# The second norm in six steps per quarter, and DVE alone draining the banks between the halves, in a two-layer flow-matching step

## The chip, the cores and the metric

The kernel runs on one core of a Trainium2 chip. The metric is the time of one execution in microseconds (us) on the device; the median of several executions counts. The engines have short names here: PE is the matrix engine (TensorE; PEld its weight loads), DVE the vector engine, ACT the scalar engine, POOL GpSimd, and SP only issues transfers. Each engine works through its own queue in order: an instruction that waits holds up everything that stands behind it in that queue.

## What is computed

Two layers of a backbone over 1,152 tokens (128 context and 1,024 latent) with a model width of 1,024. Each layer mixes the tokens (attention, gated linear attention, a recurrent unit, then an output projection) and then runs a squared-ReLU network. The change touches the end of the first sub-layer and the second one:

```python
def layer(x, cond, l, P, ctx):
    ...
    x = x + g1 * mix
    h = rmsnorm(x, P['norm2'][l]) * (1.0 + sc2) + sh2
    u = jax.nn.relu(h @ P['w_mlp1'][l])
    x = x + g2 * ((u * u) @ P['w_mlp2'][l])
    return x, new_ctx
```

`w_mlp1` is 1024 x 4096 and `w_mlp2` 4096 x 1024 per layer. All data is float32.

## The kernel before

**Layout and precision.** The residual stream x lies transposed in SBUF, as eight tiles `x` of 128 x 1152 (width block by token). A float32 product is made from three matmuls: each operand is split into a rounded high part and a low part (names ending in h and l), the high part by an ACT cast, the low part by a subtraction, mostly on DVE. So every weight block costs ACT and DVE one pass each.

**The network in two halves.** The tokens are worked through in two halves of 576, each as two sub-blocks of `TW` = 288. The up product uses a seven-product scheme (Winograd's form of Strassen's) over blocks of tokens and width: seven products of sums and differences instead of eight of blocks. So `norm2(half)` has to deliver, for each of four quarters `kk` (width blocks kk and kk+4), four normed blocks P0, P1, P3, P4, three combinations of them, and high and low parts of all seven, in the tiles `ch` and `cl`. One quarter is: multiplications by the reciprocal root (L1254, POOL, for half 0 partly DVE), scalings by gain and shift (L1256, ACT), four combinations (L1257 to L1260, POOL and DVE), and four or seven casts and as many subtractions (L1264 on ACT, L1265 on DVE). The temporaries come from two rings, `te` (five buffers) and `tn` (six), and one tile `er`.

**Up and down.** For each of 16 pairs of blocks of the hidden width, `up_prep` loads the weights and combines them (L1318 to L1321 on POOL, using one buffer `s1`) and splits them (L1299 on ACT, L1300 on DVE); `up_pair` makes the seven products (L1335 to L1337). `down` multiplies the squared activations `uh`, `ul` by `w_mlp2` (L157 to L159) into one of seven PSUM banks (five `pg`, two `pd`), and the result is added to x with the gate g2: one DVE instruction reads the bank and x and writes x (L1415). Between the two halves, after the last `up_pair` of half 0, the remaining downs of half 0 run: sixteen outputs over two hidden blocks (6 matmuls each) and sixteen over four (12 each). In this stretch (`spare`) every second output, that of sub-block `tt` = 1, is drained otherwise: ACT scales the bank into a temporary in the buffer `s1` (L1412), and POOL adds it to x (L1413).

**What sets the order.** PE's order is as the code is written. Side jobs such as `norm2` are generators in a list `chain`; at certain points of PE's program `tick()` runs the first of them on to its next `yield`, which places its instructions there. The order of the other engines' queues and of SP is set by a planner when the kernel is built, from the written order and its own forecast, so that a `yield` moves work but does not fix its place.

`norm2` runs in two places. The first is `post_out`, the tail of the output projection (L1219 to L1221, drained by DVE at L1226, weights split at L120 and L121): there the norm's statistics for token block 1 are taken (L305 to L319), `spread` turns them into a tile (L332, L337, L339), and `norm2(0)` prepares half 0. The squares of token block 2 (L305 again) follow. The second is the stretch between the halves, where `norm2(1)` is queued just ahead of the remaining downs, and `finish` runs what is left of it ahead of half 1.

Of the kernel before, what the change touches and what calls it, by code (L numbers as in the profile page):

```python
# [7 lines left out]
F32 = mybir.dt.float32  # L8
F32R = mybir.dt.float32r
AF = mybir.ActivationFunctionType  # L10
ALU = mybir.AluOpType
# [11 lines left out]
TW = 288  # L23
# [13 lines left out]
def f32(ap):  # L37
    return ap.bitcast(F32)
# [12 lines left out]
class Net:  # L51
# [1177 lines left out]
    def mlp(self, l, post_out, early, last_tb, side_work=None):  # L1229
        nc, I = self.nc, self.I  # L1230
        hg, hp = self.open(f"h2_{l}", bufs=1)
# [4 lines left out]
        def norm2(half):  # L1236
            h0 = 2 * TW * half
            pbs = []
            for tb in range(half, half + 2):
                pbs.append(((yield from self.spread(self.rs2[tb], self.tn)), tb))  # L1240
            for kk in range(4):
                P = [self.te()[:, :TW] for _ in range(3)]
                if kk % 2:
                    P += [self.tn()[:, :TW] for _ in range(4)]
                else:
                    er = hp.tile([128, 4 * TW], F32, tag="er", name="er")
                    P += [er[:, TW * i:TW * i + TW] for i in range(4)]
                for k, t, d in ((kk, 0, P[0]), (kk, 1, P[1]), (kk + 4, 0, P[3]), (kk + 4, 1, P[4])):
                    eng = nc.vector if t == 0 and half == 0 else nc.gpsimd
                    g = h0 + TW * t  # L1250
                    for pb, tb in pbs:
                        lo, hi = max(g, tb * TB), min(g + TW, tb * TB + TB)
                        if lo < hi:
                            eng.tensor_tensor(d[:, lo - g:hi - g], self.x[k][:, lo:hi], pb[:, lo - tb * TB:hi - tb * TB], ALU.mult)  # L1254
                    for a, b, s in ((0, TP, 0), (TP, TW, 1)) if g == 0 else ((0, TW, 1),):
                        nc.scalar.activation(d[:, a:b], d[:, a:b], AF.Identity, bias=M["sh2"][:, k, s:s + 1], scale=M["G2"][:, k, s:s + 1])  # L1256
                nc.gpsimd.tensor_tensor(P[2], P[4], P[1], ALU.subtract)  # L1257
                nc.vector.tensor_tensor(P[1], P[1], P[0], ALU.subtract)
                nc.vector.tensor_tensor(P[5], P[4], P[1], ALU.subtract)
                nc.gpsimd.tensor_tensor(P[6], P[3], P[5], ALU.subtract)  # L1260
                pcs = [(0, P[0]), (1, P[1]), (2, P[2])] + ([(i, P[i]) for i in range(3, 7)] if kk % 2 else [(3, er)])
                for i, r in pcs:
                    c = slice(TW * i, TW * i + r.shape[-1])
                    nc.scalar.copy(HH[kk][:, c], r)  # L1264
                    nc.vector.tensor_tensor(HL[kk][:, c], r, f32(HH[kk])[:, c], ALU.subtract)  # L1265
                yield

        post_out(lambda: self.add(norm2(0)))
        ug, up = self.open(f"u_{l}", side="right", bufs=6)
        eg, ep = self.open(f"e_{l}", bufs=1)  # L1270
        NF = DFF // 128
# [15 lines left out]
        def bank():  # L1287
            nr[3] += 1
            if nr[3] % 7 < 5:
                return self.pg()  # L1290
            return self.psp.tile([128, 512], F32, tag="pd", name="pd", bufs=2)

        def raw():
            return rot(0, RT, F32)

        def split(r, m=1024, hl=None):
            h, lo = hl or (rot(1, HT, F32R), rot(2, LT, F32R))
            h, lo = h[:, :m], lo[:, :m]
            nc.scalar.copy(h, r[:, :m])  # L1299
            nc.vector.tensor_tensor(lo, r[:, :m], f32(h), ALU.subtract)  # L1300
            return h, lo
# [85 lines left out]
            act(1, 1, o, v)  # L1387
            act(1, 0, one(4), w)

        def down(half, fs, tts=(0, 1), spare=False):  # L1390
            n = len(fs)
            wd = 256
            for d0 in range(0, D, wd):
                r = raw()
                nc.sync.dma_start(r[:, :n * wd].rearrange("p (k c) -> p k c", k=n),
                                  I["w_mlp2"][l, fs[0] * 128:fs[0] * 128 + n * 128, d0:d0 + wd].rearrange("(k p) c -> p k c", p=128))
                h, r = split(r, n * wd)
                wh, wl = (v.rearrange("p (k c) -> p k c", k=n) for v in (h, r))
                for dd in range(wd // 128):
                    dt = d0 // 128 + dd  # L1400
                    sl = slice(128 * dd, 128 * dd + 128)
                    for tt in tts:
                        p = bank()
                        self.dense(p[:, :TW], [wh[:, k, sl] for k in range(n)], [wl[:, k, sl] for k in range(n)],
                                   [tuple(v[:, TW * tt:TW * tt + TW] for v in U[f]) for f in fs])
                        self.tick()
                        c0 = 2 * TW * half + TW * tt
                        for a, b, s in ((0, TP, 0), (TP, TW, 1)) if c0 == 0 else ((0, TW, 1),):
                            xa = self.x[dt][:, c0 + a:c0 + b]
                            if spare and tt:  # L1410
                                t = hp.tile([128, 512], F32, tag="s1", name="s1")[:, :TW]
                                nc.scalar.activation(t, p[:, a:b], AF.Copy, scale=self.M[l]["g2"][:, dt, s:s + 1])  # L1412
                                nc.gpsimd.tensor_tensor(xa, xa, t, ALU.add)  # L1413
                                continue
                            nc.vector.scalar_tensor_tensor(xa, p[:, a:b], self.M[l]["g2"][:, dt, s:s + 1], xa, ALU.mult, ALU.add)  # L1415

        NPR = NF // 2
        for half in range(2):
            up_prep(0)
            for g in self.h2s:  # L1420
                self.finish(g)
            if half == 0 and side_work:
                self.add(side_work())
            for p in range(NPR):
                up_pair(p, half == 1 and p == 0)
                if half and p == NPR - 4:
                    early()
                if p == NPR - 2:
                    down(half, range(2 * p - 4, 2 * p - 2))
                elif p % 2 == 0 and p:  # L1430
                    down(half, range(2 * p - 4, 2 * p))
                if p + 1 < NPR:
                    up_prep(p + 1)
            if half == 0:
                self.h2s = [self.add(norm2(1))]
            else:
                self.drain()
                self.close(eg)
                self.close(hg)
                more[0] = False  # L1440
                last_tb(0)
            calm[0] = half == 0
            down(half, range(NF - 6, NF - 4), spare=half == 0)
            if half == 0:
                down(half, range(NF - 4, NF), spare=True)
                calm[0] = False
            else:
                for tt in range(2):
                    down(half, range(NF - 4, NF), (tt,))
                    last_tb(1 + tt)  # L1450
# [77 lines left out]
    def layer(self, l, depth):  # L1528
# [4 lines left out]
        nc = self.nc  # L1533
# [3 lines left out]
        def load_next(force):  # L1537
            if seq and seq[0] not in self.ms and (force or seq[0][1] or seq[0][0] in done):
                assert seq[0][1] or seq[0][0] in done
                self.out_load(*seq[0])  # L1540

        def out_step():
            if not state["left"]:
                if not seq:
                    return False
                load_next(True)
                state.update(cur=seq[0], gen=self.out_half(l, *seq.pop(0)), left=2 * KD)
            next(state["gen"])
            state["left"] -= 1
            if state["left"] <= 5:  # L1550
                load_next(False)
            return True
# [23 lines left out]
        def post_out(norm2):  # L1576
            done.add(2)
            load_next(False)
            for _ in rs0:
                pass  # L1580
            k = 0
            self.h2s = []
            while out_step():
                k += 1
                if not self.h2s and state["cur"] not in ((0, 0), (1, 0)):
                    self.chain.insert(0, self.norm_rs(self.xa, 1, self.rs2, eng0=nc.vector))
                    self.h2s.append(norm2())
                if k % 2 == 0:
                    self.tick()
            self.add(self.norm_rs(self.xa, 2, self.rs2, eng0=nc.vector))  # L1590
            self.close(self.kg)
            self.close(self.mg)
# [92 lines left out]
```

## Time and profile before

| | |
|---|---|
| time, median of 3 runs | 2994.66 us (2992.08 to 2997.44) |
| the profiled execution | 2993.37 us |
| its span, first to last instruction | 2991.6 us |
| mean granted clock of PE | 0.952 of full |
| busy: PE, DVE, ACT, POOL | 91%, 68%, 48%, 43% of the span |

The profile is of one execution. A busy share over the whole span says little here: the stretches around the change are short, and have rows of their own below.

### The profile page before, as it was taken

The numbers are of one execution on the slowest core, as the hardware profiler recorded it, in microseconds if no ns is written. First come the engines' busy times: TensorE is split into PE (matmuls) and PEld (weight loads), VectorE is DVE, ScalarE is ACT, GpSimd is POOL, SyncE is SP. The second block draws the span as 40 slices with busy tenths as digits, with TensorE's granted clock in tenths as the row PEclk, the third lists the DMA queues.
The fourth block names the chain that finished last, engine by engine and source line by source line (L and its number), as shares of the span: only waits on it lengthen the run. The fifth ranks groups of instructions, "written<-read, shape, count | busy, mean of one in ns | idle before, by whom it ended". The sixth has DMA issues, their size and how long they took to land. (4 is left out here: it accounts for less than half of the span.)

```text
span 2991.6 us, 49206 instructions
## 1 busy us (share of the span) xinstructions
PE 2715.6 (91%) x18377; PEld 2582.1 (86%) x18377; DVE 2046.8 (68%) x3575; ACT 1434.4 (48%) x2620; POOL 1275.1 (43%) x1292
## 2 busy tenths in 40 slices
PE   5898999979999969999888988999799996899998
PEld 3797887779999969999887878878799996899998
DVE  7645677787667757676765547778876768567676
ACT  4645457763434444343446436477543345334333
POOL 4223456754333454333223244576533336433332
PEclk8998999989999979999999999999899998999999
DMA  7544356324523223232243643752233221223223
GB/s 256 140 141 137 111 179 223 103 64 135 162 73 98 64 73 97 85 99 68 63 138 95 171 126 96 227 187 69 77 100 92 85 85 58 77 78 92 87 73 124
DMA packets 375726, 337.05 MB, mean 113 GB/s; under 512 B 32208, under 2 KB 355392, under 8 KB 375488
## 3 DMA queue, kind: packets, MB, share of 16 engines
q1 hardware_dynamic: 375272, 333.85, 36.8%
q8 instruction: 146, 2.39, 0.3%
q14 instruction: 92, 0.75, 0.1%
q10 hardware_dynamic: 216, 0.06, 0.0%
HBM read 289.93 MB, written 43.91 MB: 112 GB/s over the span
## 5 line engine op out<-in xcount | busy, mean ns | idle before, releaser
L1357 POOL TENSOR_TENSOR te<-te 128x288 f32<-128x288 f32 x256 | 187.7, 742 | 503.0 <-ACT uh L1356 494.6
L157 PE MATMUL pd<-hh,wh 128*128 128x384 f32 x816 | 296.0, 363 | 22.5 <-DVE te L492 10.7
L1415 DVE SCALAR_TENSOR_TENSOR x<-pg,mod,x 128x288 f32<-128x288 f32 (+2 forms) x492 | 206.9, 446 | 135.4 <-PE pg L159 134.3
L158 PE MATMUL pd<-hl,wh 128*128 128x384 f32 x816 | 285.6, 350 | 3.4 <-DVE hl L393 3.4
L159 PE MATMUL pd<-hh,wl 128*128 128x384 f32 x816 | 284.7, 349 | 0.0
L1299 ACT CAST wh<-wr 128x1024 fp32r<-128x1024 f32 (+1 forms) x136 | 134.9, 992 | 267.5 <-PE pg L158 147.8
L1358 DVE TENSOR_TENSOR ul<-te,uh 128x288 fp32r<-128x288 f32 x256 | 177.9, 710 | 117.8 <-POOL te L1357 115.6
L157 PE MATMUL pg<-uh,wh 128*128 128x288 f32 x788 | 234.6, 298 | 3.6 <-DVE x L1415 3.6
L159 PE MATMUL pg<-uh,wl 128*128 128x288 f32 x788 | 233.9, 297 | 0.6 <-DVE wl L1300 0.6
L158 PE MATMUL pg<-ul,wh 128*128 128x288 f32 x788 | 233.6, 296 | 0.0
L157 PE MATMUL pg<-uh,eh 128*128 128x288 f32 x680 | 202.7, 298 | 0.9 <-DVE x L1415 0.9
L159 PE MATMUL pg<-uh,el 128*128 128x288 f32 x680 | 202.8, 298 | 0.0
L158 PE MATMUL pg<-ul,eh 128*128 128x288 f32 x680 | 202.4, 298 | 0.0
L1299 ACT CAST eh<-wr 128x1024 fp32r<-128x1024 f32 (+1 forms) x108 | 109.5, 1014 | 187.2 <-PE pg L158 83.2
L1355 ACT ACTIVATE te<-te 128x288 f32<-128x288 f32 x256 | 109.8, 444 | 166.6 <-DVE te L1354 166.1
L157 PEld LDWEIGHTS pd<-hh,wh 128*128 128x128 f32 x816 | 161.9, 198 | 30.5 <-DVE te L492 11.3
L1335 PE MATMUL pg<-ch,eh 128*128 128x288 f32 x544 | 163.5, 301 | 24.3 <-ACT eh L1299 24.3
L1300 DVE TENSOR_TENSOR wl<-wr,wh 128x1024 fp32r<-128x1024 f32 (+1 forms) x136 | 159.0, 1169 | 38.6 <-ACT wh L1299 38.4
L1337 PE MATMUL pg<-ch,el 128*128 128x288 f32 x544 | 164.4, 302 | 8.0 <-DVE el L1300 8.0
L1300 DVE TENSOR_TENSOR el<-wr,eh 128x1024 fp32r<-128x1024 f32 (+1 forms) x108 | 134.0, 1241 | 47.7 <-ACT eh L1299 47.6
L158 PEld LDWEIGHTS pd<-hl,wh 128*128 128x128 f32 x816 | 161.6, 198 | 3.8 <-DVE hl L393 3.8
L1219 PE MATMUL pd<-mh,wh 128*128 128x384 f32 x384 | 141.1, 367 | 25.3 <-ACT wh L120 15.2
(384 smaller groups left out, 9499.5 us busy)
## 6 DMA issues: line engine op xcount, KB each, us to landing
wr<-in_w_mlp_dram SPq DMA_DIRECT2D x174, 512.0 KB, 3.7
wm<-in_w_mod_dram SPq DMA_DIRECT2D x96, 512.0 KB, 5.8
er<-in_w_mlp_dram SPq DMA_DIRECT2D x74, 512.0 KB, 4.2
wr<-in_w_out_dram SPq DMA_DIRECT2D x48, 512.0 KB, 4.3
wr<-in_w_in_dram SPq DMA_DIRECT2D x36, 512.0 KB, 5.2
xd<-x SPq DMA_DIRECT2D x48, 192.0 KB, 3.4
x<-xd SPq DMA_DIRECT2D x48, 192.0 KB, 4.7
raw<-mixd SPq DMA_DIRECT2D x40, 192.0 KB, 2.5
```

The lines of the kernel that those rows point to most:

```text
L157: mm(out, wh[i], xs[i][0], start=i == 0, stop=False)
L158: mm(out, wh[i], xs[i][1], start=False, stop=False)
L159: mm(out, wl[i], xs[i][0], start=False, stop=i == n - 1)
L1219: nc.tensor.matmul(p[:, :TB], wh[:, k, sl], xs[k][0], start=k == 0, stop=False)
L1299: nc.scalar.copy(h, r[:, :m])
L1300: nc.vector.tensor_tensor(lo, r[:, :m], f32(h), ALU.subtract)
L1335: mm(out, wh[:, c], HH[k][:, xs], start=k == 0, stop=False)
L1337: mm(out, wl[:, c], HH[k][:, xs], start=False, stop=k == 3)
L1355: nc.scalar.activation(r, r, AF.Relu)
L1357: nc.gpsimd.tensor_tensor(r, r, r, ALU.mult)
L1358: nc.vector.tensor_tensor(ul, r, f32(uh), ALU.subtract)
L1415: nc.vector.scalar_tensor_tensor(xa, p[:, a:b], self.M[l]["g2"][:, dt, s:s + 1], xa, ALU.mult, ALU.add)
```

## The change

Three edits. In `norm2` a `yield` stands after each of the four normed blocks and one after the four combinations, so that a quarter is six steps of the chain, where it was one. In `post_out` the chain is advanced at every step of the output projection, where it was every second. And `spare` is gone: between the halves DVE drains both sub-blocks.

```diff
--- before.py
+++ after.py
@@ -1254,10 +1254,12 @@
                             eng.tensor_tensor(d[:, lo - g:hi - g], self.x[k][:, lo:hi], pb[:, lo - tb * TB:hi - tb * TB], ALU.mult)
                     for a, b, s in ((0, TP, 0), (TP, TW, 1)) if g == 0 else ((0, TW, 1),):
                         nc.scalar.activation(d[:, a:b], d[:, a:b], AF.Identity, bias=M["sh2"][:, k, s:s + 1], scale=M["G2"][:, k, s:s + 1])
+                    yield
                 nc.gpsimd.tensor_tensor(P[2], P[4], P[1], ALU.subtract)
                 nc.vector.tensor_tensor(P[1], P[1], P[0], ALU.subtract)
                 nc.vector.tensor_tensor(P[5], P[4], P[1], ALU.subtract)
                 nc.gpsimd.tensor_tensor(P[6], P[3], P[5], ALU.subtract)
+                yield
                 pcs = [(0, P[0]), (1, P[1]), (2, P[2])] + ([(i, P[i]) for i in range(3, 7)] if kk % 2 else [(3, er)])
                 for i, r in pcs:
                     c = slice(TW * i, TW * i + r.shape[-1])
@@ -1387,7 +1389,7 @@
             act(1, 1, o, v)
             act(1, 0, one(4), w)
 
-        def down(half, fs, tts=(0, 1), spare=False):
+        def down(half, fs, tts=(0, 1)):
             n = len(fs)
             wd = 256
             for d0 in range(0, D, wd):
@@ -1407,11 +1409,6 @@
                         c0 = 2 * TW * half + TW * tt
                         for a, b, s in ((0, TP, 0), (TP, TW, 1)) if c0 == 0 else ((0, TW, 1),):
                             xa = self.x[dt][:, c0 + a:c0 + b]
-                            if spare and tt:
-                                t = hp.tile([128, 512], F32, tag="s1", name="s1")[:, :TW]
-                                nc.scalar.activation(t, p[:, a:b], AF.Copy, scale=self.M[l]["g2"][:, dt, s:s + 1])
-                                nc.gpsimd.tensor_tensor(xa, xa, t, ALU.add)
-                                continue
                             nc.vector.scalar_tensor_tensor(xa, p[:, a:b], self.M[l]["g2"][:, dt, s:s + 1], xa, ALU.mult, ALU.add)
 
         NPR = NF // 2
@@ -1440,9 +1437,9 @@
                 more[0] = False
                 last_tb(0)
             calm[0] = half == 0
-            down(half, range(NF - 6, NF - 4), spare=half == 0)
+            down(half, range(NF - 6, NF - 4))
             if half == 0:
-                down(half, range(NF - 4, NF), spare=True)
+                down(half, range(NF - 4, NF))
                 calm[0] = False
             else:
                 for tt in range(2):
@@ -1585,8 +1582,7 @@
                 if not self.h2s and state["cur"] not in ((0, 0), (1, 0)):
                     self.chain.insert(0, self.norm_rs(self.xa, 1, self.rs2, eng0=nc.vector))
                     self.h2s.append(norm2())
-                if k % 2 == 0:
-                    self.tick()
+                self.tick()
             self.add(self.norm_rs(self.xa, 2, self.rs2, eng0=nc.vector))
             self.close(self.kg)
             self.close(self.mg)
```

In the new file the lines behind the new `yield`s have numbers higher by one or two (L1258 becomes L1259, L1265 L1267, L1318 L1320, L1300 L1302), and the drain behind the removed branch a lower one (L1415 becomes L1412). The queues differ in four stretches only: the two places named above, in both layers. Three pieces of them, from layer 0, show what moved. The first is ACT at the end of the output projection; `ch_6219` is the high part of quarter 1 of `norm2`, `wh` that of the projection's weights. Before:

```order
L1256 ACTIVATE tn<-tn,mod_1_2797,G_5491 128x288
L1264 CAST ch_6219<-te 128x288
L1264 CAST ch_6219<-tn 128x288
L1264 CAST ch_6219<-te 128x288 x2
L1264 CAST ch_6219<-tn 128x288
L120 CAST wh<-wr 128x1024
L1264 CAST ch_6219<-tn 128x288 x2
L1256 ACTIVATE er<-er,mod_1_2797,G_5491 128x288
L120 CAST wh<-wr 128x1024
```

After:

```order
L1256 ACTIVATE tn<-tn,mod_1_2797,G_5491 128x160
L120 CAST wh<-wr 128x1024 x2
L1256 ACTIVATE tn<-tn,mod_1_2797,G_5491 128x288
L1266 CAST ch_6219<-te 128x288
L1266 CAST ch_6219<-tn 128x288
L1266 CAST ch_6219<-te 128x288
L1266 CAST ch_6219<-tn 128x288
L1256 ACTIVATE er<-er,mod_1_2797,G_5491 128x288
L1266 CAST ch_6219<-te 128x288
L1266 CAST ch_6219<-tn 128x288 x2
L120 CAST wh<-wr 128x1024
```

Of the two casts of weights (L120) that now stand together ahead of quarter 1's casts, the second is the one that stood in the midst of them; the first stood ahead of all of `norm2(0)`'s casts before, so it comes later now. The last row of the second piece is the cast that stood last in the first piece.

The second piece is DVE between the halves; `x_3706` to `x_3709` are x's tiles of width blocks 4 to 7, `cl_6222` and `cl_6223` the low parts of quarters 0 and 1. Before:

```order
L1265 TENSOR_TENSOR cl_6222<-er,ch_6218 128x1152
L1258 TENSOR_TENSOR te<-te 128x288
L1265 TENSOR_TENSOR cl_6223<-te,ch_6219 128x288
L1259 TENSOR_TENSOR tn<-tn,te 128x288
L1265 TENSOR_TENSOR cl_6223<-te,ch_6219 128x288 x2
L1265 TENSOR_TENSOR cl_6223<-tn,ch_6219 128x288 x4
L1415 SCALAR_TENSOR_TENSOR x_3707<-pg,mod_2_5488,x_3707 128x128
L1415 SCALAR_TENSOR_TENSOR x_3707<-pg,mod_2_5488,x_3707 128x160
L1265 TENSOR_TENSOR cl_6224<-te,ch_6220 128x288
```

After:

```order
L1267 TENSOR_TENSOR cl_6222<-er,ch_6218 128x1152
L1412 SCALAR_TENSOR_TENSOR x_3706<-pg,mod_2_5488,x_3706 128x288
L1412 SCALAR_TENSOR_TENSOR x_3707<-pg,mod_2_5488,x_3707 128x128
L1412 SCALAR_TENSOR_TENSOR x_3707<-pg,mod_2_5488,x_3707 128x160
L1412 SCALAR_TENSOR_TENSOR x_3707<-pd,mod_2_5488,x_3707 128x288
L1259 TENSOR_TENSOR te<-te 128x288
L1412 SCALAR_TENSOR_TENSOR x_3708<-pd,mod_2_5488,x_3708 128x128
L1260 TENSOR_TENSOR tn<-tn,te 128x288
L1412 SCALAR_TENSOR_TENSOR x_3708<-pd,mod_2_5488,x_3708 128x160
L1267 TENSOR_TENSOR cl_6223<-te,ch_6219 128x288 x3
L1267 TENSOR_TENSOR cl_6223<-tn,ch_6219 128x288 x4
```

The drains of blocks 4 to 6 (the rows with all 288 columns are sub-block 1, which was ACT's) now stand between the parts of quarter 1; before, the quarter was one piece, and the next drain stood behind it.

The third piece is POOL at the end of the same stretch; the `s_` tiles are the buffer `s1`. Before:

```order
L1413 TENSOR_TENSOR x_3707<-x_3707,s_11494 128x288
L1413 TENSOR_TENSOR x_3708<-x_3708,s_11531 128x288
L1413 TENSOR_TENSOR x_3709<-x_3709,s_11562 128x288
L1318 TENSOR_TENSOR s_11569<-wr 128x512
L1319 TENSOR_TENSOR wr<-er,wr 128x512
```

After:

```order
L1258 TENSOR_TENSOR te<-tn,te 128x288
L1261 TENSOR_TENSOR er<-er 128x288
L1261 TENSOR_TENSOR tn<-tn 128x288
L1320 TENSOR_TENSOR s_11537<-wr 128x512
L1321 TENSOR_TENSOR wr<-er,wr 128x512
```

The additions to x are gone, and the combination of half 1's first weights directly follows the norm's last ones. SP's transfers are the same; in layer 0 the eight stores of x for the next layer, each of which waits for a finished tile of x, stand in this stretch: before, seven of them in a row behind the loads of half 1's first weights, and now mixed with the loads of the weights after those.

## Rows read from the trace of the kernel before

**Rows 1.** The page, part 1: busy us, share of the span, instructions.

```profile
PE 2715.6 (91%) x18377; PEld 2582.1 (86%) x18377; DVE 2046.8 (68%) x3575; ACT 1434.4 (48%) x2620; POOL 1275.1 (43%) x1292
```

**Rows 2.** Waits of PE, whole span: who waited for whom: us, times, longest.

```profile
PE pd L157 <- ACT s L1412: 35.0, 2, 17.8
PE pg L1335 <- ACT eh L1299: 24.3, 6, 8.6
PE pd L1219 <- ACT wh L120: 15.2, 4, 7.2
```

**Rows 3.** Timeline of PE: start, us, instruction [idle before <-releaser].

```profile
1030.48 0.29 PE L1337 MATMUL pg<-ch,el 128*128 128x288 f32 x1
...
1065.35 0.61 PE L157 MATMUL pd<-uh,eh 128*128 128x288 f32 x1 [17.22 <-ACT s L1412]
...
1105.90 0.61 PE L1335 MATMUL pg<-ch,eh 128*128 128x288 f32 x1 [8.36 <-ACT eh L1299]
```

**Rows 4.** Windows: length, busy us (count) PE, PEld, DVE, ACT, POOL; clock; DMA.

```profile
1030.50:1067.00 36.50, 14.71 (x88) 13.95 (x87) 29.01 (x47) 22.89 (x48) 28.93 (x38) 0.67 0.15 44
1067.00:1098.00 31.00, 30.55 (x217) 30.15 (x216) 15.00 (x29) 11.22 (x18) 12.70 (x14) 0.94 0.37 113
1106.50:1113.00 6.50, 6.09 (x31) 5.84 (x30) 1.74 (x2) 0.30 (x1) 1.57 (x2) 0.62 0.37 110
612.00:673.00 61.00, 43.54 (x216) 41.12 (x215) 49.91 (x75) 36.63 (x71) 29.70 (x32) 0.85 0.22 66
```

**Rows 5.** DVE by line, 1030.5-1067 us: count | busy, mean ns | idle.

```profile
L1265 DVE TENSOR_TENSOR cl<-te,ch 128x288 fp32r<-128x288 f32 x12 | 9.5, 819 | 0.7 <-ACT ch L1264 0.7
L1265 DVE TENSOR_TENSOR cl<-tn,ch 128x288 fp32r<-128x288 f32 x5 | 4.8, 1004 | 0.0
L1415 DVE SCALAR_TENSOR_TENSOR x<-pg,mod,x 128x128 f32<-128x128 f32 (+1 forms) x10 | 3.2, 354 | 0.0
L1258 DVE TENSOR_TENSOR te<-te 128x288 f32<-128x288 f32 x4 | 3.0, 744 | 2.0 <-POOL te L1257 2.0
L1265 DVE TENSOR_TENSOR cl<-er,ch 128x1152 fp32r<-128x1152 f32 x2 | 2.7, 1360 | 1.0 <-ACT ch L1264 0.9
...
L1259 DVE TENSOR_TENSOR tn<-tn,te 128x288 f32<-128x288 f32 x2 | 1.5, 748 | 0.0
...
L1259 DVE TENSOR_TENSOR er<-er,te 128x288 f32<-128x288 f32 x2 | 1.0, 484 | 0.0
...
L1415 DVE SCALAR_TENSOR_TENSOR x<-pd,mod,x 128x128 f32<-128x128 f32 (+1 forms) x2 | 0.6, 362 | 3.2 <-PE pd L159 3.2
```

**Rows 6.** DVE by line, 1067 to 1106.5 us.

```profile
L1265 DVE TENSOR_TENSOR cl<-tn,ch 128x288 fp32r<-128x288 f32 x4 | 2.8, 748 | 0.0
...
L1300 DVE TENSOR_TENSOR wl<-er,wh 128x1024 fp32r<-128x1024 f32 x1 | 1.2, 1216 | 0.0
```

**Rows 7.** DVE by line and form, whole span.

```profile
L1415 DVE SCALAR_TENSOR_TENSOR x<-pg,mod,x 128x288 f32<-128x288 f32 x284 | 143.2, 511 | 97.3 <-PE pg L159 96.3
```

**Rows 8.** ACT and POOL by line, 1030.5 to 1106.5 us.

```profile
L1412 ACT ACTIVATE s<-pg,mod 128x288 f32<-128x288 f32 x12 | 6.0, 499 | 15.2 <-PE pg L159 10.1 <-POOL x L1413 5.0
...
L1413 POOL TENSOR_TENSOR x<-x,s 128x288 f32<-128x288 f32 x16 | 15.9, 994 | 18.3 <-ACT s L1412 18.3
```

**Rows 9.** Timelines of ACT, then POOL, between layer 0's halves.

```profile
1064.81 0.49 ACT L1412 ACTIVATE s<-pd,mod 128x288 f32<-128x288 f32 x1
...
1053.46 1.00 POOL L1413 TENSOR_TENSOR x<-x,s 128x288 f32<-128x288 f32 x1
...
1097.42 0.79 POOL L1413 TENSOR_TENSOR x<-x,s 128x288 f32<-128x288 f32 x1 [2.37 <-ACT s L1412]
1098.29 1.26 POOL L1318 TENSOR_TENSOR s<-wr 128x512 f32<-128x512 f32 x1
```

**Rows 10.** DVE by line, 612 to 673 us.

```profile
L305 DVE TENSOR_TENSOR tn<-tn 128x384 f32<-128x384 f32 x5 | 3.7, 766 | 0.0
```

**Rows 11.** The page, part 6: transfers: xcount, KB each, us to landing.

```profile
wr<-in_w_mlp_dram SPq DMA_DIRECT2D x174, 512.0 KB, 3.7
```

## The prediction

> **What bounds the kernel now.** PE is busy for 91% of the span [rows 1], so over most of it PE sets the time, and only stretches in which PE stands still can give anything back. The second view to read is therefore the list of PE's own waits, sorted by total. Three of its lines lie in the stretches that the change touches [rows 2]: 35.0 us in two waits on ACT's drain L1412 (one in each layer, between the halves), 24.3 us in six waits for weights `eh` (8.6 us at most), and 15.2 us in four waits for the output projection's `wh` (7.2 us at most). The first is the change's own line.
>
> Third comes PE's timeline between the halves of layer 0 [rows 3]: the last up product of half 0 starts at 1030.48, PE stands still for 17.22 us until 1065.35, and again for 8.36 us until 1105.90, where half 1's products that need the combined weights go on. The windows [rows 4] show that it is not lack of hands: up to 1067 us DVE was busy for 29.0 of 36.5 us, POOL for 28.9, PE for 14.7, at a clock of 0.67; from 1067 on PE runs through at 0.94.
>
> The cause of the first standstill is seen where ACT and POOL meet [rows 9]. The second addition to x ran on POOL at 1053.46, in the midst of the norm's work, and the next drain followed on ACT only at 1064.81, behind the casts of two quarters of `norm2(1)`. All banks were full by then. The second standstill has a tail of the same cause: the last addition, at 1097.42, holds the buffer `s1`, and POOL's combination of half 1's first weights starts at 1098.29, right behind it.
>
> **Between the halves, step by step.** Removed are 16 drains per layer on ACT (499 ns) and 16 additions on POOL (994 ns) [rows 8]; added are 16 drains on DVE at 511 ns, the mean of the same instruction elsewhere [rows 7], 8.2 us per layer. PE no longer depends on ACT and POOL for its banks; it depends on DVE's order alone. So I make the sum on DVE, up to the split of the first weights of the long downs (the `wl` row, 1.2 us [rows 6]), on which the last sixteen outputs wait.
>
> The four quarters of `norm2(1)` cost DVE 9.5 + 4.8 + 3.0 + 2.7 + 1.5 + 1.0 = 22.5 us up to 1067 [rows 5] and 2.8 after it [rows 6], 25.3 in all, about 12.65 for two. In the new order two quarters stand ahead of that split, not nearly four: 22.5 - 12.65 = 9.85 us leave this part. Twelve drain pieces of sub-block 0 ran there before (3.2 + 0.6 us for six outputs [rows 5], 0.63 each); now it is eight outputs, 1.3 us more, and eight of sub-block 1 at 0.51, 4.1 us. So DVE has 29.0 - 9.85 + 1.3 + 4.1 + 1.2 = 25.8 us of work. Its idle time there was 36.5 - 29.0 = 7.5 us [rows 4], partly waits for POOL, ACT and PE [rows 5]. I keep it whole: the steps are finer, but the links between the engines remain. The long downs then start at 1030.5 + 25.8 + 7.5 = 1063.8.
>
> They are 16 outputs of 12 matmuls. Before, 217 matmuls took 31.0 us at a clock of 0.94 [rows 4], or 0.134 us each at full clock; 192 take 25.8 us. The clock will have fallen once more by then (PE still waits in the first part), which took 6% of the 31 us, 1.9 us. PE is done at 1063.8 + 27.7 = 1091.5. By then DVE has the other two quarters (12.65), the 16 drains (8 x 0.63 + 8 x 0.51 = 9.1) and seven splits of about 1.2 (8.5) behind it: 30.3 us against PE's 27.7, but the last splits are not wanted at once by half 1, so I count PE's end. `s1` is free, POOL has no additions, and the weights of half 1 are combined while the downs run. So half 1 goes on at about 1091.5 where it stood until 1105.9 [rows 3]: **14.4 us**. The clock of 0.62 in the 6.5 us that followed the standstill [rows 4] goes too: 0.38 x 6.5 = **2.5 us**. Together 16.9 us per layer.
>
> Costed at nothing: ACT and POOL lose 8 and 16 us, and neither is on the path any more. PE's matmuls and the transposes of the spread keep their places here. SP's stores of x in layer 0 wait for drains that now come no later; if a load of the weights after them stands behind a late store, that costs up to its landing, 3.7 us [rows 11], once. Nothing is queued behind on ACT, since no drain is left there.
>
> Both ends: if DVE never idled, PE or DVE's whole work would be the limit, 29.0 + 15.0 [rows 4] + 8.2 = 52.2 us from 1030.5, so 1082.7: 23.2 + 2.5 = 25.7 us. If the idle time doubled, 16.9 - 7.5 = 9.4 us.
>
> On the drains a rule speaks against the change. The Trainium skill, "TensorEngine Tiling (Array Packing)", section PSUM Bottleneck, says that both ScalarE and VectorE should be used to evacuate PSUM. By it alone the change would cost 16 x 0.51 = 8.2 us of DVE per layer and give nothing, some 3011 us. The trace differs here: ACT's drain alone is as fast as DVE's (499 against 511 ns), but it drains into a buffer that POOL must empty, and what PE waited for was that chain.
>
> **The tail of the output projection.** Here nothing is added or removed; the same instructions are issued earlier and in smaller pieces. The transposes for the statistics and the spread come 18 to 36 matmuls earlier on PE. From 612 to 673 us DVE was busy for 49.9 of 61 us [rows 4]: it is nearly the bound, so of PE's waits (7.2 us for `wh`, and others) only what DVE idles can come back, 11.1 us. I take half, 5.5, since what starts earlier on DVE still waits on POOL and ACT in the chain of a quarter. The five additions of the squares of token block 2, 3.7 us [rows 10], stood partly ahead of the splits that half 0 waits for and now stand behind; they must be done soon after, so half again, 1.9. Together **7.4 us** per layer; ends 0 and 11.1 + 3.7 = 14.8. One wait is new: the first weights of the last projection block are now cast behind quarter 0's casts, so PE will stand there earlier, instead of the 7.2 us that it stood later.
>
> **The sum.** 16.9 + 7.4 = 24.3 us per layer, 48.6 for two. The profiled execution took 2993.4 us (span 2991.6 and 1.8 around it), so 2944.8; the median of the runs shown is 1.3 above it: **2946 us**.
>
> **Rivals.**
> - *PE-paced.* The finer steps take the idle time out of DVE altogether. For it: DVE's idle time was mostly waits of 1 to 3 us, at the heads of quarters [rows 5]; against it: those links are all still there. Gains at their upper ends, 25.7 + 14.8 = 40.5 per layer: 2994.7 - 81 = 2914 us.
> - *Half of it.* The banks come free, but DVE waits for the norm's links twice as long, since more of its work stands between them, and the projection's tail gives nothing, DVE being full there. For it: the cast and subtraction of a quarter go through three engines. 9.4 per layer: 2976 us.
> - *Slower: DVE takes the stall over.* All seven banks now hang on one queue in which some 30 instructions of `norm2(1)` wait for POOL or ACT. If DVE waited out all that POOL does in the first part, 28.9 us [rows 4] instead of 7.5, the gain of 16.9 would be a loss of 4.5; the same in the projection's tail, the idle 11.1 us twice, -11.1: 15.6 per layer, 3026 us. It decides once the waits added exceed 24.3 us per layer. Against it: POOL's work would have to be hardly overlapped with DVE's, and DVE has 24 drains in the first part that do not depend on POOL. For it: DVE's subtractions ran at 819 and 1004 ns while POOL was busy and 748 later [rows 5, 6]. On this the Trainium skill, "SBUF — State Buffer", section Who interferes with whom, says that a DVE instruction with two SBUF inputs and a GpSimd one that reads SBUF shut each other out for a whole instruction; the slowed rows agree.
> - That the change does not do what it says is ruled out by the queues: drains do stand between the parts of a quarter.
>
> **Chances.** Forecast 0.56, its own range 2930 to 2966. PE-paced 0.14. Half of it 0.19. Within 0.2% (6 us, about what a measurement can tell from no change) 0.04. Slower 0.07. So faster 0.89, same 0.04, slower 0.07. The range 2912 to 2980 leaves out some 0.05 below (the fastest third of the PE-paced case) and 0.15 above (a slow end of the half case, no change, slower).
>
> **What would show it.** Right: the wait of PE on L1412 by ACT is gone with both its 17 us; half 1's products go on about 60 us after the last up product of half 0, not 75; the second wait on `eh` is under 2 us; DVE is the fullest engine between the halves, at over 0.8. In the projection's tail the wait for `wh` is shorter, and half 0 starts some 7 us sooner. Wrong: a wait of PE on the drain by DVE of over 10 us at one place; DVE idle for more than 15 us in the first part; or half 1 still waiting on POOL's combination.

## The result, and the profile after

The changed kernel takes **2948.4 us** (median of 4 runs, 2947.9 to 2950.19), the kernel before on the same chip 2993.51 us: ratio 0.9848, 95% interval 0.9831 to 0.9865. The forecast was 2946 us. The page of the profile after, part 1, answers to [rows 1]; DVE has 4 us more, ACT 15 and POOL 24 less:

```profile
PE 2703.5 (92%) x18377; PEld 2570.7 (87%) x18377; DVE 2051.1 (70%) x3607; ACT 1419.2 (48%) x2588; POOL 1251.2 (42%) x1260
```

PE's waits over the whole span, for [rows 2] (us in total, times, longest). The 35.0 us on ACT's drain and the 8.4 us waits for half 1's weights are gone, and so are the 15.2 us for the projection's `wh`. New are waits for the long downs' weights (L157, L159) and two of 8.0 us at the transposes L314; a further 8.3 us of that line stood there before, elsewhere.

```profile
PE pe L314 <- DVE tn L307: 24.0, 4, 8.0
...
PE pg L159 <- DVE wl L1302: 12.0, 3, 5.8
...
PE pg L1339 <- DVE el L1302: 10.6, 4, 2.7
...
PE pd L1219 <- DVE x L1226: 8.4, 4, 3.2
...
PE pg L157 <- ACT wh L1301: 7.2, 2, 4.1
```

PE's timeline between layer 0's halves, for [rows 3]: the first down behind half 0's last up product, the two waits that are left, half 1's first up product, and its first down. (For the same up product in the kernel before, the row is the second fence's.)

```profile
1029.62 0.29 PE L157 MATMUL pg<-uh,wh 128*128 128x288 f32 x1
...
1050.54 0.61 PE L157 MATMUL pg<-uh,wh 128*128 128x288 f32 x1 [3.13 <-ACT wh L1301]
1057.05 0.61 PE L159 MATMUL pg<-uh,wl 128*128 128x288 f32 x1 [5.66 <-DVE wl L1302]
...
1085.12 0.30 PE L1337 MATMUL pd<-ch,wh 128*128 128x288 f32 x1
...
1126.08 0.29 PE L157 MATMUL pd<-uh,eh 128*128 128x288 f32 x1
```

```profile
1096.59 0.30 PE L1335 MATMUL pd<-ch,wh 128*128 128x288 f32 x1
```

These starts cut the stretch in two. Part A runs from the first down behind half 0's last up product to half 1's first up product, part B from there to half 1's first down. Windows over A and B, before and then after (columns as in [rows 4]). Two more rows of the kernel after follow: A up to the second wait, and the first 6.5 us of B.

```profile
1030.60:1096.60 66.00, 44.21 (x297) 43.29 (x296) 43.99 (x75) 33.61 (x65) 41.01 (x49) 0.79 0.25 77
1096.60:1148.10 51.50, 38.55 (x254) 37.27 (x253) 30.75 (x42) 21.65 (x38) 26.64 (x23) 0.87 0.28 86
```

```profile
1029.60:1085.10 55.50, 44.20 (x296) 43.41 (x295) 47.61 (x89) 29.19 (x53) 32.62 (x38) 0.85 0.28 84
1085.10:1126.10 41.00, 36.70 (x255) 36.00 (x254) 28.77 (x46) 18.63 (x34) 20.32 (x18) 0.92 0.38 119
1029.60:1057.00 27.40, 16.15 (x106) 15.36 (x104) 23.23 (x49) 18.46 (x36) 21.57 (x29) 0.80 0.12 39
1085.10:1091.60 6.50, 6.50 (x51) 6.50 (x50) 3.12 (x8) 1.05 (x1) 4.08 (x3) 1.00 0.83 261
```

So layer 0 gained 10.5 us in A and 10.5 in B, 21.0 in all. In layer 1 the two parts together went from 118.1 to 95.2 us by the same starts, 22.9 less.

The projection's tail is the other place. In layer 0 the network's first up product came 44.3 us after the first of the tail's matmuls (53.7 before), but the first down came after 93.6 us (96.4 before): 9.3 us gained and 6.5 given back. In layer 1 the first down came 92.3 us after (93.0 before). PE's rows there, the third in the first pair of the network, and the windows from the tail to the first down, before and after:

```profile
653.17 0.41 PE L1219 MATMUL pd<-mh,wh 128*128 128x384 f32 x1 [3.24 <-DVE x L1226]
665.76 0.40 PE L1339 MATMUL pg<-ch,el 128*128 128x288 f32 x1 [2.60 <-DVE el L1302]
675.36 0.87 PE L314 MATMUL pe<-ident,tn 128*128 128x128 f32 x3 [8.02 <-DVE tn L307]
```

```profile
612.10:708.50 96.40, 78.13 (x455) 74.00 (x454) 79.85 (x139) 52.16 (x100) 49.32 (x49) 0.88 0.26 76
```

```profile
614.70:708.20 93.50, 75.39 (x454) 71.57 (x453) 79.81 (x141) 52.54 (x102) 50.95 (x49) 0.89 0.27 82
```

### The profile page after: what moved, and what is told of

Read it like the earlier page. It is cut to its first block, busy times and chain, and to the rows that moved or that the text cites. A ratio compares the mean times of both kernels' runs of the same rounds, so it can differ in the third digit from the quotient of the medians.

```text
span 2946.9 us, 49164 instructions
## 1 busy us (share of the span) xinstructions
PE 2703.5 (92%) x18377; PEld 2570.7 (87%) x18377; DVE 2051.1 (70%) x3607; ACT 1419.2 (48%) x2588; POOL 1251.2 (42%) x1260
## 5 line engine op out<-in xcount | busy, mean ns | idle before, releaser
L157 PE MATMUL pd<-hh,wh 128*128 128x384 f32 x816 | 295.8, 363 | 23.3 <-DVE te L492 10.7
L1412 DVE SCALAR_TENSOR_TENSOR x<-pg,mod,x 128x128 f32<-128x128 f32 (+1 forms) x516 | 218.2, 449 | 122.8 <-PE pg L159 122.1
L159 PE MATMUL pd<-hh,wl 128*128 128x384 f32 x816 | 284.4, 349 | 0.0
L159 PE MATMUL pg<-uh,wl 128*128 128x288 f32 x788 | 236.0, 299 | 12.1 <-DVE wl L1302 12.0
L157 PE MATMUL pg<-uh,wh 128*128 128x288 f32 x788 | 236.5, 300 | 7.2 <-ACT wh L1301 7.2
L157 PE MATMUL pg<-uh,eh 128*128 128x288 f32 x680 | 201.1, 296 | 1.3 <-DVE x L1412 1.3
L159 PE MATMUL pg<-uh,el 128*128 128x288 f32 x680 | 201.2, 296 | 0.0
L157 PEld LDWEIGHTS pd<-hh,wh 128*128 128x128 f32 x816 | 161.4, 198 | 31.4 <-DVE te L492 11.3
L1302 DVE TENSOR_TENSOR wl<-wr,wh 128x1024 fp32r<-128x1024 f32 (+1 forms) x136 | 158.6, 1166 | 32.6 <-ACT wh L1301 32.3
L1302 DVE TENSOR_TENSOR el<-wr,eh 128x1024 fp32r<-128x1024 f32 (+1 forms) x108 | 135.4, 1254 | 48.3 <-ACT eh L1301 48.3
L159 PEld LDWEIGHTS pg<-uh,wl 128*128 128x128 f32 x788 | 150.9, 192 | 13.2 <-DVE wl L1302 13.2
```

Of the source, the lines that this page charges most:

```text
L157: mm(out, wh[i], xs[i][0], start=i == 0, stop=False)
L159: mm(out, wl[i], xs[i][0], start=False, stop=i == n - 1)
```

## The experiments

All runs in one table. A and B are layer 0's parts, from the same starts in each run's timeline of PE; ratios are to the kernel before on the same chip. The planner orders the queues anew for each run, so an edit acts through its own lines and through the order that the planner makes of them.

| run | us | ratio (95%) | A | B |
|---|---|---|---|---|
| before | 2993.5 to 2995.1 | 1 | 66.0 | 51.5 |
| after | 2948.4 | 0.9848 (0.9831 to 0.9865) | 55.5 | 41.0 |
| DVE drains, whole quarters | 2976.6 | 0.9934 (0.9917 to 0.9951) | 68.0 | 40.9 |
| fine steps, ACT and POOL drain | 2982.6 | 0.9955 (0.9940 to 0.9970) | 59.8 | 50.8 |
| both, tail as before | 2953.7 | 0.9858 (0.9841 to 0.9874) | 54.2 | 42.8 |
| tail alone | 2992.7 | 0.9991 (0.9982 to 1.0001) | 65.9 | 51.8 |
| three buffers | 2992.8 | 0.9993 (0.9983 to 1.0003) | 66.6 | 50.5 |
| three buffers, fine steps | 2977.7 | 0.9936 (0.9920 to 0.9952) | 59.2 | 49.1 |
| DVE drains, quarters spaced | 2965.3 | 0.9898 (0.9882 to 0.9914) | 62.2 | 40.0 |
| after, and POOL's load back | 2975.0 | 0.9940 (0.9925 to 0.9954) | 57.8 | 52.4 |
| after, weights ahead | 2953.8 | 0.9865 (0.9850 to 0.9880) | 59.3 | 40.7 |
| after, statistics later | 2951.9 | 0.9854 (0.9833 to 0.9874) | 54.3 | 40.8 |
| after, fewer additions | 2945.7 | 0.9836 (0.9819 to 0.9852) | 54.2 | 42.6 |
| after, combinations on DVE | 2942.6 | 0.9829 (0.9815 to 0.9842) | 53.4 | 40.0 |

### One part at a time

**The drains alone.** The kernel before, with:

```diff
-            down(half, range(NF - 6, NF - 4), spare=half == 0)
+            down(half, range(NF - 6, NF - 4), spare=False)
...
-                down(half, range(NF - 4, NF), spare=True)
+                down(half, range(NF - 4, NF), spare=False)
```

> The kernel before, with the one edit that DVE drains both sub-blocks between the halves; norm2 in whole quarters, the projection's tail as before. My theory (the chain ACT, s1, POOL held the banks, and fine steps are needed so that drains on DVE don't queue behind whole quarters): both 17 us waits of PE on ACT's drain go, but a wait of PE on DVE's drain of 5 to 10 us per layer stands in their place: 10 to 14 us gained per layer, 2966 to 2974 us. Rival 1 (the drain alone does it, the planner finds the order anyway): 21 us per layer, about 2951. Rival 2 (the fine steps alone do it): a wait on DVE of about 17 us instead, 2988 to 2998.

2976.6 us, but not as any of the three theories had it. PE's timeline has a standstill as long as the old one at nearly the same time, on another tile, the first weights of the long downs:

```profile
1068.39 0.61 PE L157 MATMUL pg<-uh,wh 128*128 128x288 f32 x1 [17.28 <-ACT wh L1299]
```

ACT's timeline of this run shows that cast behind the casts of the norm's quarters. In the kernel before it ran at the same time, behind one more drain (second fence) and 2.7 us after the drain that PE had waited for [rows 9]. Two things had stood ready to stop PE in this place, and the list of waits names only one.

```profile
1066.96 0.43 ACT L1264 CAST ch<-te 128x288 fp32r<-128x288 f32 x1
1067.29 1.04 ACT L1299 CAST wh<-wr 128x1024 fp32r<-128x1024 f32 x1
```

```profile
1067.06 0.50 ACT L1412 ACTIVATE s<-pg,mod 128x288 f32<-128x288 f32 x1 [0.54 <-POOL x L1413]
1067.46 1.04 ACT L1299 CAST wh<-wr 128x1024 fp32r<-128x1024 f32 x1
```

A is no shorter (68.0 against 66.0). The whole gain is in B, where the 8.36 us are gone.

**The fine steps alone.** Before, with `if half: yield` at the two new places of `norm2`.

> The kernel before, with the finer steps in norm2 for half 1 only; ACT and POOL still drain every second output between the halves. My theory: the drains of ACT come no longer behind two whole quarters, but s1 still waits for POOL, which is full: the wait on L1412 shrinks to some 10 us per layer, 5 to 10 us gained per layer, 2974 to 2984 us. Rival (the steps alone do it): the wait goes below 3 us, about 2951. Rival (the drain alone does it): no change, 2990 to 2996.

2982.6 us, inside the expected range. A falls to 59.8; B stays. PE's rows: what is waited for in A is again the cast, which now stood on ACT behind a drain that waited for POOL, and B's wait is unchanged.

```profile
1066.97 0.61 PE L157 MATMUL pg<-uh,wh 128*128 128x288 f32 x1 [13.85 <-ACT wh L1303]
...
1104.15 0.61 PE L1339 MATMUL pg<-ch,eh 128*128 128x288 f32 x1 [8.36 <-ACT eh L1303]
```

**Both, without the tail.** After, with `if half: yield` in `norm2` and the chain at every second step in `post_out`.

> The kernel after, with the output projection's tail as before (coarse steps in norm2 for half 0, the chain at every second step). My theory: the gain of 21 to 23 us between the halves stays, the tail was worth 0 to 5 us per layer: 2948 to 2958 us. Rival (the tail gives the predicted 7.4 us per layer): 2963.

2953.7 us. The two parts alone gave 18.6 and 12.6 us, 31.2 together; with both it is 41.4. The 10 us more come from A: with whole quarters the drains bring nothing there, with fine steps they take it from 59.8 to 54.2. B gives a little back: it is 42.8, where it was 40.9 with the drains alone.

**The tail alone.** Before, with `if half == 0: yield` in `norm2` and the chain at every step.

> The kernel before, with the finer steps in norm2 for half 0 and the chain advanced at every step of the output projection, nothing changed between the halves. My theory (half 0 starts some 9 us sooner per layer, of which 6 to 9 are lost again at the wait for token block 2's statistics): 0 to 5 us gained per layer, 2985 to 2994 us. Rival (the tail gives the predicted 7.4 us per layer): 2979.

2992.7 us; the interval of the ratio holds 1. Against the run without the tail, the kernel after is 0.001 lower in ratio, less than either interval. The tail is worth a few us in all, if anything. The stretch from the tail to layer 0's first down agrees: 95.0 to 96.5 us in the seven kernels with the old tail, 93.3 to 94.1 in the five with the new tail and nothing else changed in it. In layer 1 the two groups overlap (92.4 to 93.7 and 92.1 to 93.3).

### What in the old drain cost the time

**Three buffers.** Before, with the temporaries of ACT's drains over three buffers (`h1` and `l1` hold parts of the up weights at other times):

```diff
-                                t = hp.tile([128, 512], F32, tag="s1", name="s1")[:, :TW]
+                                tag = ("s1", "h1", "l1")[dt % 3]
+                                t = (hp if dt % 3 == 0 else ep).tile([128, 512], F32, tag=tag, name=tag)[:, :TW]
```

> The kernel before, with the temporaries of ACT's drains between the halves rotating over three buffers instead of one. My theory (the drains and the long downs' weights stand behind whole quarters in ACT's queue, whatever buffer they write): the first standstill stays at 14 to 18 us, the second shrinks by up to 5: 2983 to 2996 us. Rival (the single buffer made the drains wait): the first standstill falls to under 8 us, 2958 to 2975 us.

**The same with the fine steps.**

> As the run with the fine steps for half 1 alone, and the temporaries of ACT's drains over three buffers. Theory (there ACT waited for POOL's additions with the weights' cast behind the waiting drain): the wait of 13.9 us on that cast falls to 5 to 8 us, the one of 8.4 us on half 1's weights by some 4: 8 to 12 us per layer less than 2982.6, so 2958 to 2967 us. Rival (POOL, over 0.8 busy, is itself late, so that the buffers only let ACT run ahead): 2976 to 2984 us.

2992.8 and 2977.7 us. With whole quarters the buffer was not the cause: 17.83 us stay in PE's timeline of that run (first fence). With fine steps it is worth 5 us at most (the two intervals overlap), far from the expected 16 to 25 and inside the rival's range; the wait for the cast only falls from 13.85 to 11.55 (second fence), and B is hardly shorter though its wait fell from 8.36 to 4.90. In both runs the combination of half 1's first weights stood on POOL behind the last addition but one, not behind the last.

```profile
1066.66 0.61 PE L157 MATMUL pd<-uh,eh 128*128 128x288 f32 x1 [17.83 <-ACT l L1413]
...
1104.51 0.61 PE L1335 MATMUL pg<-ch,eh 128*128 128x288 f32 x1 [4.90 <-ACT eh L1299]
```

```profile
1061.92 0.61 PE L157 MATMUL pg<-uh,wh 128*128 128x288 f32 x1 [11.55 <-ACT wh L1303]
...
1097.50 0.61 PE L1339 MATMUL pg<-ch,eh 128*128 128x288 f32 x1 [4.90 <-ACT eh L1303]
```

**POOL's load put back.** After, with as many additions on POOL as were removed, but behind DVE's drains, not ahead of any bank:

```diff
+            if extra:
+                z = hp.tile([128, 512], F32, tag="s1", name="s1")[:, :TW]
+                nc.gpsimd.memset(z, 0.0)
...
                             nc.vector.scalar_tensor_tensor(xa, p[:, a:b], self.M[l]["g2"][:, dt, s:s + 1], xa, ALU.mult, ALU.add)
+                        if extra and tt:
+                            nc.gpsimd.tensor_tensor(z, xa, z, ALU.add)
```

> The kernel after, and POOL adds each sub-block-1 piece of x, once DVE has drained it, to a spare sum in the buffer s1 between the halves: the load of the removed additions without their place in the drain. Theory (POOL's load was part of the price: it delays the norm's quarters, slows DVE, and holds half 1's first combination back): 5 to 10 us per layer more, 2958 to 2968 us, with a wait for half 1's weights of 3 to 8 us back. Rival (only ACT's queue and the chain ahead of the banks mattered): 2946 to 2953 us.

2975.0 us: 26.6 of the 45 us are lost again, more than expected. A is only 2.3 us longer, B 11.4, and as long as before. PE's row, and POOL's timeline ahead of it: the last addition waits for the last drain, and half 1's first combination stands behind it in POOL's queue, as it did in [rows 9]. The spare sum lies in `s1`, which the combination writes, so this run does not tell the place in the queue from the buffer. In the kernel after the combination started at 1072.15 (third fence), 13 us ahead of half 1.

```profile
1098.12 0.61 PE L1337 MATMUL pg<-ch,eh 128*128 128x288 f32 x1 [8.38 <-ACT eh L1301]
```

```profile
1089.64 0.79 POOL L1417 TENSOR_TENSOR s<-x,s 128x288 f32<-128x288 f32 x1 [2.38 <-DVE x L1415]
1090.51 1.26 POOL L1320 TENSOR_TENSOR s<-wr 128x512 f32<-128x512 f32 x1
```

```profile
1072.15 1.63 POOL L1320 TENSOR_TENSOR s<-wr 128x512 f32<-128x512 f32 x1 [3.05 <-DMA wr<-in_w_mlp_dram]
```

**Whole quarters, spaced.** The run with the drains alone, and in `norm2`, behind the last `yield` of a quarter:

```diff
+                for _ in range(5 * half):
+                    yield
```

> DVE drains both sub-blocks, norm2(1) in whole quarters as in the run with the drains alone, but with five empty steps behind each quarter, so that the quarters spread over the downs as the fine steps do. Theory as it stands after the first four runs (the 17.3 us wait was for the long downs' first weights, whose cast stood behind all four quarters on ACT; it now stands behind a little over two): the wait falls to 4 to 8 us, 2951 to 2961 us. Rival (small pieces are needed, since drains on DVE queue behind whole quarters): PE waits over 8 us on a drain or on the cast, 2965 to 2978 us.

2965.3 us, at the lower edge of the rival's range and with its sign: PE waits over 8 us on the cast. On a drain, which was the rival's reason, it waits 0.9 us at most. The cast no longer stands behind all four quarters, and the one wait of 17.3 us has become two, for the high and the low part of the weights, both longer than in the kernel after (3.13 and 5.66). The later place of the quarters gives 5.8 us of A (68.0 to 62.2), the small pieces 8 more (62.2 to 54.2), of which B takes 2.8 back (40.0 to 42.8).

```profile
1059.56 0.61 PE L157 MATMUL pg<-uh,wh 128*128 128x288 f32 x1 [8.31 <-ACT wh L1301]
...
1068.59 0.61 PE L159 MATMUL pg<-uh,wl 128*128 128x288 f32 x1 [8.19 <-DVE wl L1302]
```

### What is left, and why the tail gave so little

**Weights ahead.** After, with the loading and splitting of a down's weights as a function `load`, and in the second step of the short downs:

```diff
+                wh, wl = pre if pre and d0 == 0 else load(fs, d0)
+                if ahead and d0 == wd:
+                    nxt = load(ahead, 0)
```

> The kernel after, with the first weights of the long downs loaded and split in the midst of the short downs. Theory (between the halves DVE is near its bound, 47.6 of 55.5 us busy, so that what is split sooner is paid by a drain or a split that comes later): 0 to 3 us per layer, 2942 to 2950 us. Rival (the two waits of 3.1 and 5.7 us that are left between the halves go whole, nothing takes their place): 2929 to 2935 us.

2953.8 us, above both theories: no gain, and A 3.8 us longer than after. The waits at the weights moved: to the short downs (2.01 and 2.27) and to the second weights of the long ones.

```profile
1068.34 0.61 PE L159 MATMUL pg<-uh,el 128*128 128x288 f32 x1 [4.59 <-DVE el L1302]
```

**Statistics later.** After, with `norm_rs` waiting nine steps instead of two ahead of the transposes of token block 2.

> The kernel after, with the transposes for token block 2's statistics seven steps of the chain later on PE. My theory (in the kernel after, the first MLP pair stands still 8.0 us per layer at those transposes, because the squares they wait for were pushed behind norm2(0) on DVE): the wait goes below 2 us and most of it is kept, 5 to 8 us per layer, 2932 to 2940 us. Rival (DVE is the bound there, so that PE waits for the next weights or squared activations instead): 2944 to 2951 us.

**Fewer additions.** After, with `if not (tb == 2 and eng0 is nc.vector):` ahead of the additions in `squares`.

> The kernel after, leaving out the six additions of the squares of token block 2 in the output projection's tail (5.0 us of DVE per layer; that block's statistics are not the reference's). Theory A (from the tail to the first downs the amount of DVE's work is what bounds, 79.8 of 93.5 us): 4 to 6 us per layer, 2936 to 2941 us. Theory B (what bounds is the way through the engines, not the amount): the wait at the statistics' transposes shrinks and others grow, 0 to 2 us per layer, 2944 to 2950 us.

2951.9 and 2945.7 us; neither differs from the kernel after by more than the intervals. My theory of the tail falls: the 8.02 us wait is gone in both, but from the tail to the first down layer 0 took 95.3 and 94.9 us, against 93.6. Other waits of PE took its place, for the low parts of the next pairs' weights; in the run with the statistics later:

```profile
682.78 0.61 PE L1339 MATMUL pg<-ch,wl 128*128 128x288 f32 x1 [3.18 <-DVE wl L1302]
...
701.53 0.40 PE L1339 MATMUL pg<-ch,el 128*128 128x288 f32 x1 [3.72 <-DVE el L1302]
```

In layer 0, 5 us less of DVE's work brought nothing there. In layer 1 the run with fewer additions took 89.7 us for the same stretch, against 92.3 after, so the amount of DVE's work is not ruled out; the run with the statistics later took 95.3 there. What paces these pairs stays open; that the way of their weights through POOL, ACT and DVE does is argued, not shown.

**Combinations on DVE.** After, with `ce = nc.vector if half else nc.gpsimd` making the two combinations that POOL makes.

> The kernel after, with the two combinations of each quarter of norm2(1) that POOL makes given to DVE: 7.8 us per layer less on POOL between the halves, 8 subtractions of 0.45 to 0.75 us more on DVE. Theory (POOL's load carries the price: 32 additions of about 1 us cost 26.6 us in the run before, 0.83 us each): 6.5 us per layer less for POOL, 3.6 to 6 more for DVE, so 0 to 3 us per layer gained, 2942 to 2949 us. Rival (DVE, 47.6 of 55.5 us busy, is the bound now, and POOL has slack since the additions went): 3.6 to 6 us per layer lost, 2955 to 2961 us.

2942.6 us, at the lower edge of the first theory. It is the lowest time of all, and A and B are 2.1 and 1.0 us shorter than after. Its ratio, 0.9829 (0.9815 to 0.9842), overlaps that of the kernel after: faster than before is shown, faster than after is not.

## Why the prediction was right

**The sum.** Forecast 24.3 us per layer; the stretches named give 23.7: 21.0 and 22.9 between the halves where 16.9 stood, 2.8 and 0.7 in the tail where 7.4 stood. The whole kernel gained 45.1 us, 22.6 per layer; the rest lies outside these stretches, where single executions differ by as much (layer 0's tail begins at 612.1 us before and 614.7 after, with the same code up to it). The two sizes were off in opposite directions, so that 2946 is closer than its working deserved: that is luck.

**Between the halves, the sum on DVE.** It held in form, and its size was off in A. The 14.4 us of the forecast run to 1105.9, which lies 9.3 us behind half 1's first up product (1096.59). So they stand for 5.1 us in A and 9.3 in B, with the clock's 2.5 for 11.8 in B; found were 10.5 in each. The first weights' split was put at 33.3 us behind the start (25.8 of work, 7.5 idle); it took 27.4, of which DVE worked 23.2 and idled 4.2 (third row of the windows after). Keeping the old idle time whole was the larger error. Part of the difference in work is the norm's subtractions, which ran at 720 and 597 ns where 819 and 1004 stood in [rows 5]. DVE's groups up to that split:

```profile
L1267 DVE TENSOR_TENSOR cl<-te,ch 128x288 fp32r<-128x288 f32 x6 | 4.2, 720 | 1.2 <-ACT ch L1266 1.2
...
L1267 DVE TENSOR_TENSOR cl<-tn,ch 128x288 fp32r<-128x288 f32 x4 | 2.2, 597 | 0.0
```

The long downs then took 28.1 us (1057.0 to 1085.1) for 27.7 forecast, and the clock was 1.00 in the 6.5 us that followed (fourth row), where 0.62 had stood.

**The cause of the first standstill: wrong in part.** The prediction named ACT's drain. The run with the drains alone shows that taking the drain away gives A nothing, since the cast of the long downs' weights stood in the same queue behind the same quarters. That the sum came out is owed to its end point, the split of these weights, which is right for either cause. What shortened A was the work of the norm spread over more steps (59.8 with the old drains), and the drains on DVE only on top of that.

**The second standstill** was called a tail of the same cause, the last addition. That is right, and its size nearly so (10.5 found, 11.8 forecast). The run with POOL's load back loses 11.4 of B with the banks drained by DVE, so it is the additions themselves, by their place in the queue or by `s1`, not the drain's chain. Not all of the wait is the last addition's: behind the last but one it was still 4.90.

**The tail of the projection: the term that failed.** That DVE's idle time and the squares would each give back half was not so: 2.8 and 0.7 us where 7.4 stood. The early start came (9.3 us), but in layer 0 PE lost 6.5 us of it in the first pairs. The 8.02 us wait at the transposes is where it was lost in this kernel, but not why, since the time stayed lost in layer 0 when that wait was gone; the cause is open. The wait for `wh` that was called new did not come; PE waits 3.24 us on DVE's drain there. The prediction counted the gain at half 0's start; it should have been counted at the first down.

**The rivals.** PE-paced did not come: DVE still idled, and 8.8 us of waits are left in A. Half of it did not: DVE idled less, not twice as long. DVE taking the stall over is seen in a small way, as the 5.66 us on its split. On the Trainium skill's rule in "TensorEngine Tiling (Array Packing)", section PSUM Bottleneck, the measurement decides: with fine steps, both engines draining took 2977.7 us even with three buffers, DVE alone 2953.7. On the exclusion that the Trainium skill states in "SBUF — State Buffer", section Who interferes with whom, the trace agrees: in A of the kernel after, the nine of the twenty subtractions L1267 (128 x 288) that ran with no POOL instruction beside them took 444 to 459 ns, and each of those over 460 had one beside it. That it was the 16 additions that slowed them is not shown: of the ten over 1000 ns in [rows 5], four ran beside an addition, the others beside the norm's own work on POOL. The signs named were seen: no wait on ACT's drain, half 1 55.6 us after half 0's last up product, no wait for weights at its start, DVE busy for 47.6 of 55.5 us, and in the tail no wait for `wh`.

## What to carry to other kernels

A wait names one thing. Before crediting its removal, look at what stands next in the same queue: here the weights' cast, 2.7 us behind the drain, stopped PE just as long once the drain was gone. A small job given to an idle engine costs where its last piece stands, not what it takes: additions of 0.8 us, tied to the last banks, held the next half's weights back until PE had waited 8.4 us for them. And a gain at the start of a stretch counts only if it is still there at the stretch's end.

## What was not expected of the hardware

One form of DVE's subtraction (128 x 288, two operands in SBUF) took between 450 and 1004 ns on average, by what POOL did beside it. The row is of the kernel after, 1057 to 1085 us, where POOL worked for 11.1 of 28.0 us and three of the four ran with no POOL instruction beside them; that of [rows 5] is the 1004.

```profile
L1267 DVE TENSOR_TENSOR cl<-tn,ch 128x288 fp32r<-128x288 f32 x4 | 1.8, 450 | 0.3 <-ACT ch L1266 0.3
```
